# Hybrid decoder layer on one core: weight and block splits on VectorE, block sums among the products, and earlier loads of the linear attention's values

## The chip, the cores and the metric

One core of a Trainium2 chip runs the whole layer. Its engines work side by side, each through its own list of instructions in order: TensorE (PE in the profile, its weight loads PEld) does matrix products, VectorE (DVE), ScalarE (ACT) and GpSimd (POOL) work on elements, SyncE (SP) issues the transfers. The metric is the device time of one execution in microseconds.

## The reference

One token mixer layer on 1024 tokens of width 1024, in float32:

```python
h = rms_norm(x, norm_w)
proj = h @ w_in          # a_q a_k a_v a_gate | b_q b_k b_v b_gate b_low | two merge gates
oa = sliding_window_attention(rope(a_q), rope(a_k), a_v, sinks) * silu(a_gate)
ob = rms_norm(gated_linear_attention(b_q, b_k, b_v, log_a), b_out_norm_w) * silu(b_gate)
merged = sigmoid(m_a) * (oa @ w_a_proj) + sigmoid(m_b) * (ob @ w_b_proj)
out = rms_norm(x + merged @ w_out, final_norm_w)
```

The sliding attention has 16 heads of 64 and a window of 128; the linear attention has 4 heads with keys of 128 and values of 256.

## The kernel before

**Precision.** Every float32 operand of a large product is split into a rounded part h (a cast, ScalarE) and a rest l = x - h (a subtraction on GpSimd or VectorE). A product is then three matmuls: h by h, h by l, l by h. `split_w` (L114) does this for weights, with the rest on GpSimd (L116); `split_block` (L904) for blocks of activations, with the cast in L905 and the rest in L906.

**Stages.** Norm, transposes and first merge gate tiles (to about 80 us); projections of b_q, b_k, b_v, b_gate and one merge gate by `seven_products` (to about 400); sliding attention (to about 725); linear attention for heads 0 and 1, `gla(0)`, and 2 and 3, `gla(2)` (to about 880), with projection tiles `ya` of w_a_proj as fillers; w_b_proj in four calls of `seven_products`, k = 0 to 3, 128 columns of each half of the output at a time (about 913 to 990); w_out in two calls, h = 0 and 1, with residual and final norm (to the end at 1106.7).

**seven_products** (L423) multiplies 2 x 2 blocks with seven products instead of eight. Its weights are the four quadrants a11 to a22; its activations come as seven block sums (`tset`), which are split beforehand. Before, each product has its own PSUM bank `sj`; VectorE carries the running sums u and u3 (`add`, L449 to 451) and closes the four quadrants (`give`, L458 to 462); after each quadrant `emit` follows: for w_b_proj `merge` (L983, L984: gate times value, plus ya), for w_out `norm`. The four weight sums (L479 to 482, in place) stand after the third product. `part` splits a weight quadrant right before its product. With 128 columns (w_b_proj) the products are those of `half_product` (L132), with 256 (w_out) those of `token_product` (L420).

**Block sums.** `block_sums` (L908) makes the seven sums and splits them: for ob, the linear attention's output, five of them before the last `ya` tiles and the other two (L951 to 956) right before w_b_proj; for w_b_proj's own output `merged` (tiles o4 to o7) all seven after the last call, L990 and 991, five with their rest on GpSimd.

**Linear attention.** Each `gla_step` loads its values vr (L820), splits them (vh by ScalarE, L768; vl by GpSimd, L769) and multiplies (L774). Its pools, `hpv` of vr, vh, vl among them, are opened after the sliding attention has closed its own. The gates bg (L800) are loaded by `gla_loads` ahead of the steps. Three merge gate tiles (`m_tiles`) are put among the sliding attention's last steps (L757), one more among the steps of gla(0): `pace` (L861) ties a group of three filler matmuls to each step.

**Order.** The order of each engine's list is made by the compiler's scheduler (`schedule_with_timeline_sim`), within the limits of pools, banks and `issue_after`.

## Time and profile before

| | us |
|---|---|
| runs: 1113.48, 1111.57, 1110.83; median | 1111.57 |
| profiled execution, own time | 1108.61 |
| span of the profiled execution | 1106.7 |
| PE busy | 1027.7 (93%) |
| DVE busy | 774.7 (70%) |
| POOL busy | 684.3 (62%) |
| ACT busy | 542.4 (49%) |
| mean granted TensorE clock | 0.979 |

The profile page divides the span into 40 slices of 27.7 us and gives each engine's busy share in tenths; the timeline lists single instructions with start, duration and, in brackets, how long the engine was idle before and which instruction ended that. A TensorE that is busy 93% of the time leaves 79 us of idle time, and on top of it the time at a lower granted clock.

### The profile page before, as it was taken

How to read it: one execution, taken by the hardware profiler on the slowest of the kernel's cores; microseconds unless marked ns; L12 is line 12 of the kernel's file. 1: busy time of each engine (PE TensorE's matmuls, PEld its weight loads, DVE VectorE, ACT ScalarE, POOL GpSimd, SP SyncE). 2: the span in 40 equal slices, each digit the busy share in tenths (PEclk: the TensorE clock that was granted, in tenths of full speed). 3: DMA queues.
4: the chain of work that ended last, by engine and by line, in shares of the span. 5: the costliest groups of instructions: out<-in, count | busy, mean ns of one | idle time of the engine just before them, and what ended most of it. 6: DMA issues, size and time to landing. Idle time of an engine off the chain costs nothing.

```text
span 1106.7 us, 16321 instructions
## 1 busy us (share of the span) xinstructions
PE 1027.7 (93%) x5544; PEld 873.9 (79%) x5544; DVE 774.7 (70%) x1241; ACT 542.4 (49%) x1312; POOL 684.3 (62%) x542
## 2 busy tenths in 40 slices
PE   4999999899999999999999999988999997994896
PEld 3786787688889997888888878777788886873896
DVE  5999887335564323489788788748755299899766
ACT  6345865333342214556666666557654143243444
POOL 6033555777985446578677567747744246688685
PEclk9999999999999999999999999989999998996999
DMA  7332443452424152222222124266644587531315
GB/s 256 87 114 68 144 160 119 142 188 95 131 98 127 65 153 60 65 69 68 68 83 78 49 77 132 82 206 206 219 148 152 194 253 238 171 115 57 124 50 190
DMA packets 126403, 141.07 MB, mean 127 GB/s; under 512 B 10352, under 2 KB 87024, under 8 KB 126320
## 3 DMA queue, kind: packets, MB, share of 16 engines
q1 hardware_dynamic: 126320, 140.03, 40.5%
q8 instruction: 44, 0.72, 0.3%
q14 instruction: 39, 0.32, 0.1%
HBM read 95.04 MB, written 40.24 MB: 122 GB/s over the span
## 4 chain that ended last, share of the span: by engine, by line
PE 60%; DVE 16%; POOL 8%; issue 6%; ACT 6%; DMA 4%; SPq 1%; POOLq 0%; DVEq 0%; ACTq 0%
PE pj L132 22%; PE sj L132 15%; PE sj L420 11%; POOL wl L116 3%; PE sc L689 2%; PE av L729 2%; PE av L774 2%; POOL b L906 2%; DMA r<-sp_ob 1%; POOL o L906 1%; ACT wh L115 1%; PE pt L713 1%; PE sc L774 1%; DVE u L523 1%; DMA gt<-sp_cum 1%
## 5 line engine op out<-in xcount | busy, mean ns | idle before, releaser
L132 PE MATMUL pj<-o,wh 128*128 128x512 f32 x1088 | 353.6, 400 | 2.5 <-ACT o L204 1.9
L132 PEld LDWEIGHTS pj<-o,wh 128*128 128x128 f32 x1088 | 200.8, 190 | 44.2 <-ACT o L204 2.1
L116 POOL TENSOR_TENSOR wl<-wr,wh 128x1024 fp32r<-128x1024 f32 (+1 forms) x76 | 167.4, 2211 | 107.5 <-ACT wh L115 99.7
L116 POOL TENSOR_TENSOR wl<-sraw,wh 128x512 fp32r<-128x512 f32 (+1 forms) x98 | 155.3, 1600 | 107.6 <-ACT wh L115 105.5
L132 PE MATMUL pj<-o,wl 128*128 128x512 f32 x544 | 215.6, 396 | 0.0
L132 PEld LDWEIGHTS pj<-o,wl 128*128 128x128 f32 x544 | 102.5, 188 | 21.6
L115 ACT CAST wh<-wr 128x1024 fp32r<-128x1024 f32 (+1 forms) x76 | 66.9, 890 | 93.3 <-PE pj L132 23.9
L132 PE MATMUL sj<-o,wh 128*128 128x512 f32 x352 | 110.5, 395 | 0.7 <-ACT u L467 0.7
L451 DVE TENSOR_TENSOR u<-u,sj 128x512 f32<-128x512 f32 x72 | 49.2, 683 | 72.0 <-PE sj L420 40.5
L115 ACT CAST wh<-sraw 128x512 fp32r<-128x512 f32 (+1 forms) x98 | 63.2, 678 | 57.2 <-PE sj L420 29.1
L420 PE MATMUL sj<-wh,b 128*128 128x256 f32 x320 | 62.2, 296 | 21.7 <-ACT b L905 14.7
L132 PEld LDWEIGHTS sj<-o,wh 128*128 128x128 f32 x352 | 65.9, 187 | 16.9 <-ACT u L467 1.1
L420 PEld LDWEIGHTS sj<-wh,b 128*128 128x128 f32 x320 | 52.8, 203 | 23.1 <-ACT b L905 15.1
L132 PE MATMUL sj<-o,wl 128*128 128x512 f32 x176 | 69.4, 394 | 0.0
L721 POOL TENSOR_TENSOR ch<-ph,cst 128x512 fp32r<-128x512 f32 x32 | 38.4, 1201 | 48.4 <-ACT ph L720 36.0
L704 ACT ACTIVATE sm<-sc,nm 128x129 f32<-128x129 f32 x128 | 45.8, 368 | 37.4 <-DVE nm L700 36.4
L132 PE MATMUL sj<-b,wh 128*128 128x512 f32 x160 | 51.0, 402 | 5.6 <-ACT wh L115 5.6
L420 PE MATMUL sj<-wh,o 128*128 128x256 f32 x320 | 55.2, 277 | 0.1
L420 PEld LDWEIGHTS sj<-wh,o 128*128 128x128 f32 x320 | 48.4, 188 | 0.4 <-ACT wh L115 0.3
L420 PE MATMUL sj<-wl,b 128*128 128x256 f32 x160 | 45.8, 293 | 0.2 <-POOL wl L116 0.2
L609 POOL TENSOR_TENSOR qs<-qs,sin 128x512 f32<-128x512 f32 x18 | 25.4, 1409 | 31.0 <-DMA qs<-q 31.0
L420 PE MATMUL sj<-wl,o 128*128 128x256 f32 x160 | 44.3, 277 | 0.0
(314 smaller groups left out, 2737.3 us busy)
## 6 DMA issues: line engine op xcount, KB each, us to landing
sraw<-in_w_in_dram SPq DMA_DIRECT2D x32, 512.0 KB, 4.0
wr<-in_w_in_dram SPq DMA_DIRECT2D x26, 512.0 KB, 4.0
r<-sp_ob SPq DMA_DIRECT2D x28, 256.0 KB, 4.3
qs<-q SPq DMA_DIRECT2D x72, 64.0 KB, 2.0
xt<-in_x_dram SPq DMA_DIRECT2D x8, 512.0 KB, 8.6
sp_ma<-gt SPq DMA_DIRECT2D x16, 256.0 KB, 2.0
sp_mb<-c SPq DMA_DIRECT2D x16, 256.0 KB, 2.0
gt<-sp_cum SPq DMA_DIRECT2D x16, 256.0 KB, 3.7
```

The source lines that it names most:

```text
L115: nc.scalar.copy(h, raw)
L116: nc.gpsimd.tensor_sub(l, raw, h.bitcast(F32))
L132: nc.tensor.matmul(p, a[:, k, :], b[:, k, :], start=start and k == 0 and y == 0, stop=stop and k == 3 and y == 2)
L420: nc.tensor.matmul(p, m[i][:, k, t * P : t * P + P], w[j][:, k, :], start=k == 0 and y == 0, stop=k == 3 and y == 2)
L451: nc.vector.tensor_add(o[b], like(u[b], o[b]), like(x[b], o[b]))
L609: nc.gpsimd.tensor_mul(qs, qs, sin[:, sl])
L689: nc.tensor.matmul(s[:, h * 256 : h * 256 + 256], lq, kk[kv][x][:, k0 : k0 + 2, :].rearrange("p n t -> p (n t)"), start=x == 0, stop=x == 1)
L704: nc.scalar.activation(sm[:, j, :], sel[j // 2][:, j % 2, :], AF.Exp, bias=nm[:, j : j + 1], accum_out=den[:, j : j + 1])
L721: nc.gpsimd.tensor_mul(ch, ph.bitcast(F32), leb)
L729: nc.tensor.matmul(av[:, b * 256 : b * 256 + 256], val[:, blk, kv, :], part[:, 2 * b : 2 * b + 2, :], start=y == 0, stop=y == len(terms) - 1)
L774: nc.tensor.matmul(p, a[i], b[j], start=start and y == 0, stop=stop and y == 2)
L906: (eng or nc.vector).tensor_sub(m[1][:, k, :], r, f(m, 0, k))
```

## The change

- `split_w` takes its rest engine from `rest`: GpSimd until the first `ya` tiles, VectorE from then on. The splits of blocks and the norm's multiplications by `fnw` are on VectorE, too.
- `seven_products` splits three weight quadrants first, makes the four weight sums right behind them, and splits the others one product ahead. Where an `order` is given (w_b_proj and w_out), products 3 and 5 add onto product 1's bank and 7 onto 4's; ScalarE copies the bank after 1, 3 and 5 (u1, u3, u5), and VectorE only closes the quadrants. Without it (the projections) the sums are those of before.
- `after` is called behind each product: `last_blocks` during k = 0 of w_b_proj, `sums` (merged's block sums, slices 0 to 2, slice 3 where ready) during k = 3.
- w_out's halves of rows are swapped, and the residual is added in `norm` for three of four quadrants.
- `hpv` is opened before the sliding attention; two merge gate tiles instead of three stand in its last steps, and two instead of one in gla(0), with six filler matmuls a step.

```diff
+    rest = [nc.gpsimd]
     def split_w(raw, h, l):
         nc.scalar.copy(h, raw)
-        nc.gpsimd.tensor_sub(l, raw, h.bitcast(F32))
+        rest[0].tensor_sub(l, raw, h.bitcast(F32))
...
+        w = {i: part(r, n) for i, r in ((1, a11), (2, a12), (6, a22))}
         nc.vector.tensor_add(a22, a21, a22)
         nc.vector.tensor_sub(a21, a11, a21)
         nc.vector.tensor_sub(a11, a22, a11)
         nc.vector.tensor_sub(a12, a12, a11)
-        add(u, u, product(a11, t2))
-        u3 = tiles("u3")
-        add(u3, u, product(a21, t3))
-        for b in range(nb):
-            nc.vector.tensor_add(c[b], c[b], like(u3[b], c[b]))
-            emit(c[b], 1, 0, b)
-        x = product(a22, t1)
-        add(u, u, x)
-        earlier(u3, 1, 1)
-        give(1, 1, u3, x)
-        earlier(u, 0, 1)
-        if not fine:
-            give(0, 1, u, product(a12, b22))
+        by = {1: (b11, a11), 2: (b21, a12), 3: (t2, a11), 4: (t1, a22), 5: (t3, a21), 6: (t4, a22), 7: (b22, a12)}
+        x, u = {}, {}
+        def like(p, o):
+            return p.rearrange("p (t c) -> p t c", t=2) if len(o.shape) == 3 else p
+        def product(i, b):
+            if n == P:
+                half_product(x[i][b], w[i], by[i][0], not order or i not in (3, 5, 7), not order or i not in (1, 3, 4))
...
+        def ahead(i):
+            if i not in w:
+                w[i] = part(by[i][1], n)
+        def alone(i, following=None):
+            ahead(i)
+            x[i] = [bank("sj") for b in range(nb)]
+            for b in range(nb):
+                product(i, b)
+            if following:
+                ahead(following)
...
+        for i in order:
+            ahead(i)
+            x[i] = x[{3: 1, 5: 1, 7: 4}[i]] if i in (3, 5, 7) else [bank("sj") for b in range(nb)]
+            if i == 7 and fine:
+                break
+            for b in range(nb):
+                product(i, b)
+            if i in (1, 3, 5):
+                u[i] = [u_pool.tile([P, 512], F32, name=f"u{i}") for b in range(nb)]
+                for b in range(nb):
+                    nc.scalar.copy(u[i][b], x[i][b])
+                    if i == 3 and early:
+                        early(u[i][b], 0, 1, b)
+            if i == 2:
+                give(0, 0, 1, 2)
+            if i in (4, 5) and 4 in x and 5 in u:
+                give(1, 1, 5, 4)
+            if i in (5, 6) and 6 in x and 5 in u:
+                give(1, 0, 5, 6)
+            if i == 7:
+                give(0, 1, 3, 7)
+            if after:
+                after(i)
...
+    hpv = c3.enter_context(pool_of(name="hpv", bufs=4))
...
-                for _ in range(3):
+                for _ in range(2):
...
-    pace += [steps[min(15, 2 + i)] for i in range(16 * len(fillers))]
+    pace += [steps[min(15, 2 + i // 2)] for i in range(16 * len(fillers))]
...
+    rest[0] = nc.vector
+    up_ = lctx.enter_context(pool_of(name="up2", bufs=2))
+    sr = lctx.enter_context(pool_of(name="sr2", bufs=2))
...
+    def last_blocks(i):
+        if i < 3:
+            for k in (2 * i - 2, 2 * i - 1):
+                r11, r12 = (raw_block(k, 0, th) for th in range(TH))
+                nc.vector.tensor_sub(r12, r12, r11)
+                split_block(ob[5], k, r12)
+        if i == 3:
+            for k in range(4):
+                split_block(ob[6], k, raw_block(k, 1, 1))
...
+    def sums(i):
+        y = {1: 0, 2: 1, 3: 3, 4: 5, 5: 4, 6: 2, 7: 6}[i]
+        mt[y] = block(y)
+        def diff(k):
+            t2s.append(rp.tile([P, 512], F32, name="r"))
+            nc.vector.tensor_sub(t2s[k], c12[k], c21[k])
+            nc.vector.tensor_sub(c11[k], c11[k], t2s[k])
+        if i == 2:
+            split_block(mt[1], 3, c11[3])
+        if i == 6:
+            split_block(mt[0], 3, c21[3])
+            nc.vector.tensor_sub(c21[3], c22[3], c21[3])
+            split_block(mt[5], 3, c21[3])
+        for k in range(3):
+            if i == 3:
+                nc.vector.tensor_sub(c21[k], c22[k], c21[k])
+                diff(k)
+            if i == 5:
+                nc.vector.tensor_sub(c22[k], c12[k], c22[k])
+            if i < 7:
+                split_block(mt[y], k, {0: c21, 1: c11, 2: c11, 3: t2s, 4: c22, 5: c21}[y][k])
+        if i == 7:
+            diff(3)
+            split_block(mt[3], 3, t2s[3])
+            split_block(mt[2], 3, c11[3])
+            nc.vector.tensor_sub(c22[3], c12[3], c22[3])
+            split_block(mt[4], 3, c22[3])
+            for k in range(4):
+                split_block(mt[6], k, c12[k])
...
+                       lambda a, th, b: mg[a][th][:, k, :], merge, range(1, 8), after={0: last_blocks, 3: sums}.get(k))
...
-            nc.sync.dma_start(w[i, a], w_out[i * 512 : i * 512 + 512, c : c + 256].rearrange("(k p) c -> p k c", p=P))
+            nc.sync.dma_start(w[i, a], w_out[512 - i * 512 : 1024 - i * 512, c : c + 256].rearrange("(k p) c -> p k c", p=P))
...
+            if a == 1 or th == 0:
+                residual(o, a, th, b)
...
-                    nc.gpsimd.tensor_mul(o[:, t, :], o[:, t, :], fnw[:, cs])
-        seven_products([[w[i, a] for a in range(2)] for i in range(2)], mt, 256, up_,
+                    nc.vector.tensor_mul(o[:, t, :], o[:, t, :], fnw[:, cs])
...
+                       (1, 2, 6, 3, 5, 4, 7) if h else (1, 2, 4, 6, 3, 5, 7), early=residual, fine=h == 1)
```

How the order moves, at three places. First SP, the transfers, before: end of the sliding attention (oa is its output, written to sp_oa; bg the gates and vr the values of the linear attention; wr weights; sp_ma merge gate tiles).

```order
L308 DMA sp_ma_72<-gt_7009 128x512
L741 DMA sp_oa_70<-oa_6740 128x512
L800 DMA bg_7098<-sp_bg_77 128x2x512
L308 DMA sp_ma_72<-gt_7037 128x512
L800 DMA bg_7110<-sp_bg_77 128x2x512
L820 DMA vr_7122<-sp_bv_76 128x256
L820 DMA vr_7162<-sp_bv_76 128x256
L820 DMA vr_7202<-sp_bv_76 128x256
L820 DMA vr_7249<-sp_bv_76 128x256
L800 DMA bg_7486<-sp_bg_77 128x2x512
```

Now, the same tiles vr stand at the beginning of the sliding attention, among the last writes of sp_bv and ahead of and among the rope's loads qs:

```order
L122 DMA wr_3937<-in_w_in_dram 128x8x128
L857 DMA vr_7076<-sp_bv_76 128x256
L857 DMA vr_7116<-sp_bv_76 128x256
L601 DMA sp_bv_76<-c_3606 128x2x256
L857 DMA vr_7156<-sp_bv_76 128x256
L857 DMA vr_7203<-sp_bv_76 128x256
L122 DMA wr_4227<-in_w_in_dram 128x8x128
L857 DMA vr_7250<-sp_bv_76 128x256
L857 DMA vr_7297<-sp_bv_76 128x256
L857 DMA vr_7344<-sp_bv_76 128x256
L646 DMA qs_3690<-q_3688 32x512 x4
```

and at the attention's end the list reads:

```order
L779 DMA sp_oa_70<-oa_6647 128x512
L779 DMA sp_oa_70<-oa_6759 128x512
L857 DMA vr_7464<-sp_bv_76 128x256
L837 DMA bg_7052<-sp_bg_77 128x2x512
L837 DMA bg_7064<-sp_bg_77 128x2x512
L837 DMA bg_7440<-sp_bg_77 128x2x512
L837 DMA bg_7452<-sp_bg_77 128x2x512
L857 DMA vr_7511<-sp_bv_76 128x256
```

So the first eight loads of vr have moved from behind bg to some 70 rows earlier; bg still stands behind the last write of sp_oa.

Second TensorE at the same place: pj are merge gate products, av with ph, pl, ch, cl the attention's last ones, L813 to 815 of the linear attention's first step (L850 to 852 now). Before:

```order
L132 MATMUL pj_6950<-o6_89,wl_6919 128x512
L132 MATMUL pj_6984<-o0_83,wh_6980 128x512
L132 MATMUL pj_6984<-o1_84,wh_6980 128x512
L132 MATMUL pj_6984<-o0_83,wl_6981 128x512
L729 MATMUL av_6782<-ph_6774,vv_3730 128x256
L132 MATMUL pj_6984<-o0_83,wh_6980 128x512
L132 MATMUL pj_6984<-o1_84,wh_6980 128x512
L729 MATMUL av_6724<-cl_6719,dv_3731 128x256
L729 MATMUL av_6724<-ph_6716,vv_3730 128x256
L729 MATMUL av_6724<-ch_6718,dv_3731 128x256
L729 MATMUL av_6724<-pl_6717,vv_3730 128x256
```

Now:

```order
L134 MATMUL pj_6969<-o6_89,wl_6938 128x512
L767 MATMUL av_6801<-ph_6793,vv_3749 128x256
L767 MATMUL av_6743<-cl_6738,dv_3750 128x256
L767 MATMUL av_6743<-ph_6735,vv_3749 128x256
L767 MATMUL av_6743<-ch_6737,dv_3750 128x256
L767 MATMUL av_6743<-pl_6736,vv_3749 128x256
L767 MATMUL av_6743<-cl_6738,dv_3750 128x256
L751 MATMUL pt_6840<-cst_97,sm_6818 128x128 x4
L767 MATMUL av_6801<-ch_6795,dv_3750 128x256
L767 MATMUL av_6801<-pl_6794,vv_3749 128x256
L767 MATMUL av_6801<-cl_6796,dv_3750 128x256
L767 MATMUL av_6801<-ph_6793,vv_3749 128x256
```

The merge gate matmuls that stood before and among the attention's last products are gone from there (they are fillers of gla(0) now).

Third VectorE at the end of w_b_proj and the start of w_out: o4 to o7 are merged's quadrants, b0 to b9 and o0 to o3 the split block sums, wr and wl weights. Before, behind the last quadrant of k = 3 (L461 and merge):

```order
L461 TENSOR_TENSOR o6_9495<-u_9983,sj_10098 128x512
L983 SCALAR_TENSOR_TENSOR o6_9495<-ym_10112,o6_9495 128x512
L984 TENSOR_TENSOR o6_9495<-o6_9495,yt_10113 128x512
L919 TENSOR_TENSOR t2_10153<-o7_9497,o4_9494 128x512
L917 TENSOR_TENSOR o4_9494<-o6_9495,o4_9494 128x512
L920 TENSOR_TENSOR o5_9496<-o5_9496,t2_10153 128x512
L924 TENSOR_TENSOR o6_9495<-o7_9497,o6_9495 128x512
L906 TENSOR_TENSOR b7_10129<-t2_10153,b6_10128 128x512
L906 TENSOR_TENSOR b5_10127<-o5_9496,b4_10126 128x512
L919 TENSOR_TENSOR t2_10161<-o7_9497,o4_9494 128x512
L920 TENSOR_TENSOR o5_9496<-o5_9496,t2_10161 128x512
L906 TENSOR_TENSOR b7_10129<-t2_10161,b6_10128 128x512
```

Now from the sum that closes quadrant (1,1) of k = 3 on:

```order
L459 TENSOR_TENSOR o7_9468<-u5_10113,sj_10076 128x512
L459 TENSOR_TENSOR o5_9467<-u5_10113,sj_10133 128x512
L940 TENSOR_TENSOR b9_10123<-o7_9468,b8_10122 128x512 x2
L940 TENSOR_TENSOR b5_10154<-o4_9465,b4_10153 128x512 x2
L1009 TENSOR_TENSOR r_10069<-o6_9466,o5_9467 128x512
L1023 TENSOR_TENSOR o7_9468<-o6_9466,o7_9468 128x512
```

and, after 10 more rows:

```order
L1050 TENSOR_TENSOR o5_9467<-o5_9467,yt_10148 128x512
L940 TENSOR_TENSOR b9_10123<-o7_9468,b8_10122 128x512
L1049 SCALAR_TENSOR_TENSOR o6_9466<-ym_10181,o6_9466 128x512
L940 TENSOR_TENSOR b5_10154<-o4_9465,b4_10153 128x512
L437 TENSOR_TENSOR wr_10223<-wr_10221,wr_10223 128x1024
L940 TENSOR_TENSOR b1_9999<-o5_9467,b0_9998 128x512
L1050 TENSOR_TENSOR o6_9466<-o6_9466,yt_10182 128x512
```

Before, all block sums of merged stand behind the last merge. Now most of slices 0 to 2 stand among the products (b9, b5 and b3 are late ones of them), and the split of b1, slice 3, which w_out's first product needs, is the 24th instruction behind the sum L459 (rows with x2 counted twice). From the first instruction of k = 0 to that sum VectorE has 112 instructions, two of them of 128x1024.

179 lines of the change are left out of this document (80 added, 99 removed).

## The prediction

> **What bounds the kernel now.** I read the 40 slices first, because they show where TensorE is not full.
>
> ```profile
> PE   4999999899999999999999999988999997994896
> DVE  5999887335564323489788788748755299899766
> POOL 6033555777985446578677567747744246688685
> PEclk9999999999999999999999999989999998996999
> ```
>
> TensorE is near full everywhere, so the kernel is bound by it, except at the start (slice 0), in slices 26 and 27 (about 720 to 775 us, the end of the sliding attention and the first half of the linear attention), slice 33 (913, start of w_b_proj) and slices 36 and 37 (1000 to 1050, start of w_out). VectorE is full in the last two. Second I read TensorE's timeline there for what ended each wait; the bracket gives idle time and releaser.
>
> ```profile
> 734.23 0.58 PE L774 MATMUL av<-vh,ath 128*128 128x256 f32 x1 [4.11 <-ACT vh L768]
> 919.46 2.07 PE L132 MATMUL sj<-b,wh 128*128 128x512 f32 x4 [5.64 <-ACT wh L115]
> 993.67 0.51 PE L420 MATMUL sj<-wh,b 128*128 128x256 f32 x2 [2.21 <-DVE u L451]
> 1014.01 0.79 PE L420 MATMUL sj<-wh,b 128*128 128x256 f32 x2 [12.64 <-ACT b L905]
> 1018.37 1.01 PE L420 MATMUL sj<-wh,b 128*128 128x256 f32 x3 [3.57 <-DVE b L906]
> 1027.85 0.50 PE L420 MATMUL sj<-wh,b 128*128 128x256 f32 x2 [2.03 <-ACT b L905]
> 1029.54 0.58 PE L420 MATMUL sj<-wh,b 128*128 128x256 f32 x1 [1.19 <-DVE b L906]
> ```
>
> Seven waits, 31.4 us. Third, what a wait costs behind itself, from windows of 5 us (window, PE, PEld, DVE, ACT, POOL busy, then PEclk):
>
> ```profile
> 735.00:740.00 5.00, 5.00 (x27) 4.87 (x26) 2.12 (x6) 3.46 (x12) 3.68 (x7) 0.56 1.06 330
> 750.00:755.00 5.00, 4.58 (x23) 3.95 (x23) 4.08 (x9) 3.28 (x10) 4.08 (x8) 0.69 0.39 123
> 920.00:925.00 5.00, 5.00 (x16) 3.92 (x15) 5.00 (x5) 2.20 (x4) 2.64 (x2) 0.63 0.89 262
> 1020.00:1025.00 5.00, 5.00 (x34) 5.00 (x33) 4.87 (x8) 2.48 (x4) 0.00 (x0) 0.73 0.00 0
> 1030.00:1035.00 5.00, 5.00 (x33) 5.00 (x33) 4.15 (x6) 2.95 (x4) 3.16 (x1) 0.70 0.07 15
> ```
>
> After each the granted clock is low for a window: 5 x (1 - clock) = 2.2, 1.55, 1.85, 1.35 and 1.5 us lost. The Trainium skill's page "TensorE: Matmul & The Clock Gate" (section "Why this matters for your kernels") says that only idle gaps over about 3 us bring the half clock back. The trace agrees behind 4.11 and 5.64, but the low windows at 750 and 1030 stand behind pairs of waits of which none is longer than 2.03; by the rule the new waits under 2 us that I find below cost no clock, and the sum stands; by those two windows they cost about 1.5 us, and the sum would be 1088.5.
>
> Fourth, why VectorE is late at 1000 to 1030:
>
> ```profile
> 1009.37 8.40 POOL L906 TENSOR_TENSOR o<-o,o 128x512 fp32r<-128x512 f32 x5
> 1031.84 4.57 POOL L116 TENSOR_TENSOR wl<-wr,wh 128x1024 fp32r<-128x1024 f32 x1 [12.39 <-ACT wh L115]
> ...
> 1011.55 1.75 DVE L920 TENSOR_TENSOR o<-o,t 128x512 f32<-128x512 f32 x1
> 1020.03 0.69 DVE L920 TENSOR_TENSOR o<-o,t 128x512 f32<-128x512 f32 x1
> 1020.68 0.69 DVE L906 TENSOR_TENSOR b<-t,b 128x512 fp32r<-128x512 f32 x1
> 1021.41 0.69 DVE L906 TENSOR_TENSOR b<-o,b 128x512 fp32r<-128x512 f32 x1
> 1022.02 0.68 DVE L919 TENSOR_TENSOR t<-o,o 128x512 f32<-128x512 f32 x1
> ```
>
> The same instruction of L920 takes 1.75 us while GpSimd runs its subtraction and 0.69 while GpSimd idles (nothing of its between 1019.5 and 1031.8). With GpSimd idle one starts every 0.60 to 0.73 (1020.68, 1021.41, 1022.02). This is the reading on which the forecast rests: GpSimd's work is paid twice, on its own engine and on VectorE.
>
> **The change, part by part.**
>
> *Work moved off GpSimd.* What leaves it, from its groups after 782 us (count, busy, mean ns):
>
> ```profile
> L116 POOL TENSOR_TENSOR wl<-wr,wh 128x512 fp32r<-128x512 f32 x28 | 45.3, 1634 | 33.1 <-ACT wh L115 28.5 <-DMA sp_t<-yt 4.6
> L906 POOL TENSOR_TENSOR b<-o,b 128x512 fp32r<-128x512 f32 x12 | 20.5, 1737 | 0.0
> L906 POOL TENSOR_TENSOR o<-o,o 128x512 fp32r<-128x512 f32 x8 | 13.0, 1658 | 0.0
> L1037 POOL TENSOR_TENSOR o<-o,fnw 128x256 f32<-128x256 f32 x24 | 22.0, 941 | 2.8 <-ACT zj L1033 2.8
> L906 DVE TENSOR_TENSOR b<-r,b 128x512 fp32r<-128x512 f32 x16 | 13.1, 849 | 3.7 <-ACT b L905 3.7
> L451 DVE TENSOR_TENSOR u<-u,sj 128x512 f32<-128x512 f32 x24 | 16.4, 681 | 13.8 <-PE sj L420 7.7 <-PE sj L132 6.1
> ```
>
> All four GpSimd groups, four more splits of blocks and 19 weight splits of 128x1024 go to VectorE, and GpSimd is nearly silent from w_b_proj on. On VectorE a moved 128x512 costs 0.60 to 0.73 where GpSimd needed 1.6 to 1.7; I take 0.60, and for 128x1024 twice that, 1.2. Against that, VectorE loses 24 of the sums of the 0.681 row, which the product's bank takes over; ScalarE gets 8 copies, hidden, since it is busy only 25.3 of 72 us in the row of 919.46:991.47 below.
>
> *Start of w_b_proj.* The 5.64 us wait ends with a weight cast, which waits for VectorE's weight sums:
>
> ```profile
> 917.01 1.75 DVE L481 TENSOR_TENSOR wr<-wr 128x512 f32<-128x512 f32 x1
> ...
> 919.46:991.47 72.01, 71.95 (x306) 58.58 (x306) 64.95 (x72) 25.32 (x43) 50.78 (x31) 0.97 0.56 172
> ```
>
> Such a sum at 0.60 instead of 1.75 gives 1.1 us back each, the splits ahead of it as well, and the sums now stand right behind the first splits, one product before they are needed. The second set of late block splits (L953 to 956) also moves behind w_b_proj's first products. I let the wait go with its clock: 5.64 + 1.85 = 7.5 saved, less 1.1 for one sum that may still be waited for, **6.4** (bounds 3 and 7.5: the loads of the blocks are not faster than before).
>
> *Inside w_b_proj.* Before, VectorE did 72 instructions beside TensorE's 72 us. Now merged's block sums stand among them: by the order, 112 instructions from the first of k=0 to the sum that closes quadrant (1,1) of k=3, 110 x 0.60 + 2 x 1.2 = 68 us beside the same 72. It just fits, but the margin is 4 us and VectorE works in order, so each wait for a product delays what is queued behind it, and product 7 now cannot start before that sum has read the bank that it adds to. I charge 2 us (bounds 0 and 6).
>
> *Start of w_out.* Between that closing sum and the last split of the first w_out operand (b1, slice 3) stand 24 instructions: 22 x 0.60 + 2 x 1.2 = 15.6 us. TensorE has, in the same time, product 7 and 28 matmuls of w_out's second product, at the pace of these two rows:
>
> ```profile
> 722.71 3.27 PE pj L132 x14
> 1036.46 47.41 PE sj L420 x398
> ```
>
> 12 x 0.2336 + 28 x 0.119 = 6.1 us. So TensorE waits 15.6 - 6.1 = 9.5 us in one piece, then runs cold for 1.7 (mean of the five windows above). Before: 2.21 + 12.64 + 3.57 + 2.03 + 1.19 = 21.6 idle, and behind it the clock: 1.35 and 1.5 from the windows at 1020 and 1030, and 0.6 for the five matmuls at 1014.01 and 1018.37, at half pace: 25.1. Saved 25.1 - 2 - 9.5 - 1.7 = **11.9** (bounds 4, where VectorE's interval is 0.73 and the charge 6, and 21, where TensorE finds other work). The rest of w_out has some 550 matmuls, 65 us, beside about 53 us of VectorE at the same prices (an estimate over its order): hidden. The norm's multiplications by fnw, on VectorE now, are among these 53; were that cover gone they would cost 24 x 0.4 = 10.
>
> *Attention's end and linear attention.* The chain of waits there, and the queue that issues its loads:
>
> ```profile
> 705.72 4.45 PE pj L132 x19
> ...
> 711.59 0.48 ACT ph L720
> 728.50 5.25 DMA vr<-sp_bv
> ...
> 727.09 0.37 SPq L800 DMA_DIRECT2D bg<-sp_bg  x1
> 728.50 2.31 SPq L820 DMA_DIRECT2D vr<-sp_bv  x4
> ...
> 745.00:785.00 40.00, 33.27 (x201) 27.54 (x200) 34.73 (x88) 27.56 (x89) 31.25 (x44) 0.96 0.67 218
> ```
>
> The values vr come 5.25 us after an issue at 728.50, behind the gates bg on SP. Loaded some 300 us earlier, they take the 4.11 us and its 2.2 of clock with them: 6.3. In the 40 us behind, TensorE idles 6.7 and loses 1.55 of clock at 750; one more filler tile (doubled pace, 6 matmuls or 1.4 us a step instead of 0.7) covers some 4 of these. What is late next: the tile that is gone stood in the attention's last chain. TensorE's other work is done at 710.2, and the next product needs ph, ready at 712.1: 1.9. The transposes and the bank behind it want 1.2 and 1.5 more by the same order, and the first step's own norm chain about 1.4, since its pt now follows after 15 matmuls. Together 6.0 (the last three are estimates from durations of casts and norm steps there): 6.3 + 4 - 6.0 = 4.3, and with the clock at 750 **6** (bounds 1 and 10). The bg loads still wait for the attention's last output; VectorE's first product with bg stands 13 instructions behind that output, so it may wait 0 to 2 us, in the bounds.
>
> The early loads of vr stand on SP ahead of the attention's first rope loads. Six issues take 6 x 0.58 = 3.5 (from the row of four, 2.31), if SP doesn't idle there anyway: 0 to 3.5, taken as 0, since the rope loads wait for a cast of ScalarE. The pair stage keeps its order on all engines: 0. Tail: 0.1 to 0.8 less, taken 0.3.
>
> Sum: 6.4 + 11.9 + 6 + 0.3 = 24.6. The profiled execution took 1108.6 us (span 1106.7 and 1.9 around it); 1084.0 then. The median of the runs shown, 1111.57, is 3.0 above that execution: **1087**.
>
> **Rivals.**
>
> *VectorE becomes the bound.* If its dependent sums start every 0.68 instead of 0.60, 136 of them cost 11 us more, of which the margin of 4 hides some: 7 late: 1094. For it: 24.73 of 25 us busy at 975 to 1000. Against: most neighbours in the new order work on different tiles.
>
> ```profile
> 975.00:1000.00 25.00, 22.74 (x126) 19.58 (x125) 24.73 (x18) 10.88 (x20) 25.00 (x14) 1.00 0.31 106
> ```
>
> *The slower side.* VectorE's slowness isn't GpSimd's doing and stays. Then 136 moved and old instructions at the 0.849 mean of the mixed group cost 136 x 0.25 = 34 us, less 4 of margin: 30 us against the 24.6 saved, 5 slower: 1117. It decides from an interval of 0.60 + (24.6 + 4) / 136 = 0.81. Against it the same instruction at 1.75 and 0.69. The Trainium skill's page "Perfetto Trace Analysis" (section "Optimizing Scalar/DVE Operations") advises the opposite of this change, to offload a saturated VectorE even to GpSimd, though it warns that the two share a read port; by the advice the move would end here, by the warning and by the rows at 1011.55 and 1020.03 it does not.
>
> *Nothing is won at the attention's end.* The wait for vr becomes one for ph, the banks and bg, all 6 us of it: 1093.
>
> *More is won.* TensorE's order at w_out has enough beside the splits, so that the 9.5 shrink to 3 and don't let the clock fall: 1079.
>
> **How the numbers follow.** Forecast (1081 to 1092) 0.5; VectorE the bound (to 1100) 0.2; nothing at the attention's end 0.1; more won (down to 1073) 0.14; slower side 0.04, change without effect 0.02. 1073 to 1100 leaves out about 2 in 10. A measurement of this kernel can tell some 0.3% (3.3 us) from no change; faster by more 0.93, within 0.03, slower 0.04.
>
> **What would show it.** VectorE's 128x512 subtractions near 0.69 from 913 us on and GpSimd silent there; no TensorE wait for a weight cast near 905; one wait of 6 to 11 us for a split or cast of b near 990 to 1005, in place of 12.64 and 3.57; no wait for vh, but for ph, at the attention's end. Wrong if VectorE's subtractions stay over 0.8, or if TensorE waits inside w_b_proj for VectorE by over 6 us.

## The result, and the profile after

| | before | changed |
|---|---|---|
| runs, us | 1110.33, 1110.83, 1111.57, 1113.48 | 1083.87, 1085.11, 1085.45, 1085.83 |
| median, us | 1111.20 | 1085.28 |
| profiled execution (span), us | 1108.61 (1106.7) | 1085.83 (1084.0) |
| PE busy, us | 1027.7 | 1023.3 |
| POOL busy, us | 684.3 | 528.1 |
| mean granted TensorE clock | 0.979 | 0.989 |

The ratio is 0.9762, 95% interval 0.9744 to 0.9779: faster by 25.9 us, 24.6 forecast. The same four rows of the 40 slices (27.1 us each now) as for the kernel before:

```profile
PE   4999999989999999999999999989999999996996
DVE  5999887534655421378878888877866379889786
POOL 5123555687897446756677766577853100000002
PEclk9999999999999999999999999999999999998999
```

GpSimd is silent from slice 32 (870 us) to the last, TensorE's dip at 720 to 775 is small, and of the two weak slices at 1000 to 1050 one is left (slice 36, 976 to 1003). TensorE's waits of over 1 us where the prediction's seven stood, and two others, on the changed kernel's timeline (two more, of 1.1 and 1.0 at 784 and 790, are left out):

```profile
435.69 1.12 PE L684 MATMUL pt<-cst,q 128*128 128x128 f32 x4 [4.04 <-ACT q L681]
...
717.67 0.38 PE L767 MATMUL av<-ph,vv 128*128 128x256 f32 x1 [1.05 <-ACT ph L758]
728.77 0.36 PE L811 MATMUL av<-vh,ath 128*128 128x256 f32 x1 [1.21 <-ACT kth L805]
919.51 0.74 PE L134 MATMUL sj<-b,wh 128*128 128x512 f32 x2 [1.12 <-ACT wh L117]
983.78 0.38 PE L422 MATMUL sj<-wl,b 128*128 128x256 f32 x1 [1.61 <-DVE wl L118]
990.99 0.39 PE L422 MATMUL sj<-wh,b 128*128 128x256 f32 x1 [2.12 <-DVE b L940]
998.19 0.52 PE L422 MATMUL sj<-wh,b 128*128 128x256 f32 x2 [2.09 <-ACT b L939]
1001.08 0.58 PE L422 MATMUL sj<-wh,b 128*128 128x256 f32 x1 [2.38 <-DVE b L940]
```

The wait for vh is gone. The one of 5.64 is 1.12. The 12.64 and 3.57 have become four of about 2. But at 435.69, the start of the sliding attention, a wait has grown from 0.90 to 4.04: there something was lost. The same wait before:

```profile
430.86 0.66 PE L646 MATMUL pt<-cst,q 128*128 128x128 f32 x4 [0.90 <-ACT q L643]
```

Where the time went, by the moment at which TensorE reaches the same amount of work (counted from its timelines, one profiled execution each; both hold the same 5544 matmuls, 4464 of them ahead of w_b_proj's first):

| TensorE reaches | before | changed | ahead by | since the row above |
|---|---|---|---|---|
| the end of its 2000th matmul (the attention's first tile of q) | 413.2 | 414.9 | -1.7 | -1.7 |
| the attention's first softmax transposes | 465.6 | 471.8 | -6.2 | -4.5 |
| the first matmul of w_b_proj | 888.7 | 885.4 | 3.3 | +9.5 |
| 240 matmuls of w_b_proj | 968.1 | 958.4 | 9.6 | +6.3 |
| 320 matmuls of w_b_proj | 986.3 | 977.3 | 9.0 | -0.6 |
| 200 matmuls of w_out | 1042.0 | 1018.4 | 23.5 | +14.5 |
| its last matmul | 1097.6 | 1075.3 | 22.3 | -1.2 |
| end of the span | 1106.7 | 1084.0 | 22.7 | +0.4 |

The 1.7 us of the first row are scatter between executions: in the fourteen profiled ones of this document TensorE ends its 2000th matmul between 411.9 and 415.2.

### The profile page after: what moved, and what is told of

Same layout as the page of the kernel before. It is cut to its first block, busy times and chain, and to the rows that moved or that the text cites. A ratio compares the mean times of both kernels' runs of the same rounds, so it can differ in the third digit from the quotient of the medians.

```text
span 1084.0 us, 16202 instructions
## 1 busy us (share of the span) xinstructions
PE 1023.3 (94%) x5544; PEld 870.1 (80%) x5544; DVE 768.1 (71%) x1312; ACT 546.9 (50%) x1320; POOL 528.1 (49%) x447
## 4 chain that ended last, share of the span: by engine, by line
PE 47%; DVE 14%; DMA 4%; POOL 4%; ACT 4%; issue 4%; SPq 0%; POOLq 0%; DVEq 0%; ACTq 0%
PE pj L134 16%; PE sj L422 14%; PE sj L134 9%; PE av L811 2%; PE sc L727 1%; DMA r<-sp_ob 1%; DVE b L940 1%; PE av L767 1%; ACT sm L742 1%; DVE oa L778 1%; DVE sm L750 1%; DVE sc L735 1%; DVE qb L708 1%; DVE nm L738 1%; PE sc L811 1%
## 5 line engine op out<-in xcount | busy, mean ns | idle before, releaser
L134 PEld LDWEIGHTS pj<-o,wh 128*128 128x128 f32 x1088 | 202.0, 191 | 43.6 <-ACT o L206 2.1
L117 ACT CAST wh<-wr 128x1024 fp32r<-128x1024 f32 (+1 forms) x76 | 66.9, 892 | 84.4 <-PE sj L422 23.5
L146 POOL TENSOR_SCALAR rstd<-zs 128x1 f32<-128x1 f32 x8 | 2.7, 334 | 213.4 <-DVE zs L1067 213.0
L118 POOL TENSOR_TENSOR wl<-wr,wh 128x1024 fp32r<-128x1024 f32 x29 | 72.0, 2482 | 34.8 <-ACT wh L117 31.6
L476 DVE TENSOR_TENSOR u<-u,sj 128x512 f32<-128x512 f32 x48 | 32.8, 684 | 55.1 <-PE sj L422 32.5
L459 DVE TENSOR_TENSOR c<-u,sj 128x512 f32<-128x512 f32 x48 | 32.7, 681 | 27.9 <-DMA sp_bq<-c 8.6
```

What stands on the lines that cost most here:

```text
L117: nc.scalar.copy(h, raw)
L118: rest[0].tensor_sub(l, raw, h.bitcast(F32))
L134: nc.tensor.matmul(p, a[:, k, :], b[:, k, :], start=start and k == 0 and y == 0, skip_group_check=True, stop=stop and k == 3 and y == 2)
L459: nc.vector.tensor_add(o, like(u[i][b], o), like(x[j][b], o))
L476: nc.vector.tensor_add(o[b], u[i][b], x[j][b])
```

## The experiments

Each run was compared with the kernel before on its own chip; there the latter's median was 1109.2 (first four runs), 1113.2 (next four) and 1111.1 (last four), so ratios are compared, not microseconds.

| run | median, us | ratio to before | 95% interval |
|---|---|---|---|
| changed kernel | 1085.28 | 0.9762 | 0.9744 to 0.9779 |
| values' pool as before | 1095.57 | 0.9880 | 0.9835 to 0.9924 |
| values in mid-attention | 1077.56 | 0.9720 | 0.9700 to 0.9740 |
| rests on GpSimd | 1104.25 | 0.9956 | 0.9942 to 0.9971 |
| before, rests on VectorE | 1106.43 | 0.9976 | 0.9957 to 0.9995 |
| sums written at the end | 1086.96 | 0.9771 | 0.9728 to 0.9813 |
| fillers 3 and 1 | 1086.03 | 0.9770 | 0.9736 to 0.9804 |
| running sums on VectorE | 1096.17 | 0.9861 | 0.9823 to 0.9900 |
| values mid, one group first | 1080.91 | 0.9732 | 0.9699 to 0.9765 |
| values mid, splits as needed | 1071.80 | 0.9656 | 0.9633 to 0.9680 |
| before, rests on VectorE, pool open | 1095.72 | 0.9865 | 0.9840 to 0.9889 |
| before, values mid | 1100.57 | 0.9910 | 0.9886 to 0.9934 |
| late block sums ahead | 1082.16 | 0.9746 | 0.9723 to 0.9769 |

### What the early loads win and cost

Two runs: the changed kernel with the values' pool opened behind the attention again,

```diff
-    hpv = c3.enter_context(pool_of(name="hpv", bufs=4))
...
-    hpa, bp1, bpe, bps, bp, hp = (c3.enter_context(pool_of(name=nm, bufs=n)) for nm, n in (
+    hpa, bp1, bpe, bps, hpv, bp, hp = (c3.enter_context(pool_of(name=nm, bufs=n)) for nm, n in (
```

> The changed kernel, but the pool of the linear attention's values is opened after the sliding attention again, as before. Theory (early loads delay the attention's start by about 6 us and save about as much at the linear attention's start): the wait of 4.04 us at 432 shrinks to about 0.9, a wait of about 4 us for vh returns at the linear attention's start, total 1084 to 1088. Rival (the early loads win clearly more than they cost): 1090 or more. Rival (they only cost): about 1079.

and the changed kernel with the pool early, but the loads held back on SP:

```diff
+            late.append(nc.sync.dma_start(sp_oa[i * P : (i + 1) * P, th * 512 : th * 512 + 512], oa).ins)
...
-        nc.sync.dma_start(vr, sp_bv[t * P : t * P + P, hd * BV : (hd + 1) * BV])
+        with tc.issue_after(late[6]):
+            nc.sync.dma_start(vr, sp_bv[t * P : t * P + P, hd * BV : (hd + 1) * BV])
```

> The changed kernel, but SP may issue the loads of the values only behind the write of the seventh half of the sliding attention's output (in its middle), the pool still being opened ahead. Theory (the early loads hold up the first rope transfers through SP's and ScalarE's queues): wait at 432 back to about 0.9, no wait for vh at the linear attention's start, total about 1079, 6 us below the changed kernel. Rival (the wait at 432 comes from the pool's place in memory or from the order of other work): stays at 1085.

The second came out as its theory had it: 0.9720, the best so far, with 0.91 us at the attention's start and no wait for vh. The first came out at 0.9880; the rival "win clearly more than they cost" held. Its timeline at the linear attention's start and its SP issues:

```profile
733.00 0.58 PE L810 MATMUL av<-vh,ath 128*128 128x256 f32 x1 [11.14 <-ACT vh L804]
...
714.13 11.06 SPq L778 DMA_DIRECT2D sp_oa<-oa  x2
727.03 0.89 SPq L836 DMA_DIRECT2D bg<-sp_bg  x2
727.96 1.88 SPq L856 DMA_DIRECT2D vr<-sp_bv  x4
```

The loads are issued at the same moment as before (727.96 against 728.50), behind the attention's last output, but TensorE is ready 8 us sooner, since one filler tile is gone from there. So the wait is 11.14, not 4.11: with the tile gone the early loads are needed. From the first softmax transposes to w_b_proj's first matmul TensorE takes 428.0 us here and 413.6 in the changed kernel; at the attention's start the late pool wins 4.6. The way in which they cost, in the changed kernel at the attention's start (SP and ScalarE), and below it the same instructions before:

```profile
416.69 1.72 SPq L857 DMA_DIRECT2D vr<-sp_bv  x3
418.46 1.87 SPq L646 DMA_DIRECT2D qs<-q  x3
...
415.45 0.75 ACT L805 CAST vh<-vr 128x256 fp32r<-128x256 f32 x2 [5.17 <-DMA vr<-sp_bv]
416.81 0.81 ACT L805 CAST vh<-vr 128x256 fp32r<-128x256 f32 x2 [0.61 <-DMA vr<-sp_bv]
417.52 0.58 ACT L642 COPY q<-pj 128x512 f32<-128x512 f32 x1
```

```profile
413.81 2.51 SPq L608 DMA_DIRECT2D qs<-q  x4
...
413.20 0.59 ACT L604 COPY q<-pj 128x512 f32<-128x512 f32 x1 [4.61 <-PE pj L132]
```

ScalarE's copy of q, which the first rope loads wait for, stands behind four casts of vh, and these wait for vr: 417.52 instead of 413.20. SP's rope loads stand behind three loads of vr that wait for a buffer to come free: 418.46 instead of 413.81. Of those 4.65 us, 1.7 are the scatter of the table's first row, for the copy waits for the 2000th matmul; the other 3 are the queues, and TensorE's wait grows by as much (0.90 to 4.04). The granted clock of 0.66 at 435 to 440 makes the rest of the table's 4.5 (5 x 0.34 = 1.7). From the 2000th matmul to the first softmax transposes the eight profiled executions without early loads at the attention's start need 52.4 us, and the six with them 57.0 to 58.4.

The third run of this group takes the same step alone, on the kernel before.

> The kernel before with only the loads of the linear attention's values moved to the middle of the sliding attention. Theory: the wait of 4.1 us for vh goes with its 2.2 us of clock, nothing is lost at the attention's start, 1103 to 1106 (ratio 0.993 to 0.995). Rival (something else is late there, such as the gates' loads): 1109 or more.

It gave 0.9910 (10 us), more than the 6 expected. From the attention's first softmax transposes to w_b_proj's first matmul, before, in this run and in the changed kernel (the first number behind the comma is TensorE's busy time):

```profile
465.58:888.66 423.08, 406.64 (x2231) 343.13 (x2230) 309.72 (x646) 249.08 (x796) 265.61 (x247) 0.99 0.40 123
466.79:879.88 413.09, 402.35 (x2231) 339.91 (x2230) 307.57 (x649) 247.22 (x796) 263.55 (x247) 1.00 0.41 126
471.83:885.38 413.55, 403.03 (x2232) 340.44 (x2230) 316.21 (x656) 249.05 (x792) 247.17 (x236) 1.00 0.41 127
```

In this run the stretch is 10.0 us shorter: idle time falls by 5.7 (16.4 to 10.7), and TensorE's busy time for the same matmuls by 4.3, at a higher granted clock. Expected were 4.1 and 2.2. How much of the difference is scatter stays open: three profiled executions of the changed kernel's list of instructions (two of them are runs below) need 411.5 to 414.5 us for this stretch.

### The moved filler tile

```diff
-                for _ in range(2):
+                for _ in range(3):
...
-    pace += [steps[min(15, 2 + i // 2)] for i in range(16 * len(fillers))]
+    pace += [steps[min(15, 2 + i)] for i in range(16 * len(fillers))]
```

> The changed kernel, but three filler tiles in the sliding attention's end and one in gla(0), paced as before. Theory of the prediction (the moved tile uncovers about as much as it covers): 1083 to 1088, with the waits for ph and kth at 717 and 728 smaller and the waits of the linear attention's steps at 745 to 785 larger. Rival (the second tile in gla(0) is what wins there): 1089 to 1093. Rival (it costs): 1081 or less.

0.9770, not to be told from the changed kernel. TensorE has no wait over 0.5 us at 715 to 750 there, but four of 1.0 to 2.0 between 753 and 778. From the first softmax transposes to w_b_proj's first matmul it needs 411.3 us, beside those 411.5 to 414.5. As with the prediction's 4 and 1.55 against 6.0, the tile covers about as much in one place as in the other; what it needs is that vr is there early.

### VectorE and GpSimd

The changed kernel with the rests back on GpSimd:

```diff
-    rest[0] = nc.vector
...
-        split_block(ob[3], k, t2)
+        split_block(ob[3], k, t2, nc.gpsimd)
...
-                    nc.vector.tensor_mul(o[:, t, :], o[:, t, :], fnw[:, cs])
+                    nc.gpsimd.tensor_mul(o[:, t, :], o[:, t, :], fnw[:, cs])
```

(and so for five of merged's seven block sums).

> The changed kernel, but the weight rests, the block rests that were GpSimd's before and the norm's multiplications stay on GpSimd. Theory (GpSimd's work slows VectorE, and its moving away is what shortens the start of w_out): VectorE's 128x512 subtractions at up to 1.7 us again, waits at the start of w_b_proj and w_out grow, total 1098 to 1108. Rival (the place of the block sums among the products is what wins, not the engine): 1083 to 1090, since VectorE would have less to do.

0.9956: 21 us of the 26 are gone. Its VectorE, GpSimd and TensorE at w_out's start:

```profile
976.88 1.75 DVE L1008 TENSOR_TENSOR r<-o,o 128x512 f32<-128x512 f32 x1
981.90 4.49 DVE L1050 TENSOR_TENSOR o<-o,yt 128x512 f32<-128x512 f32 x2
986.31 0.68 DVE L1009 TENSOR_TENSOR o<-o,r 128x512 f32<-128x512 f32 x1
...
978.05 5.04 POOL L940 TENSOR_TENSOR o<-o,o 128x512 fp32r<-128x512 f32 x3
987.11 1.61 POOL L940 TENSOR_TENSOR b<-o,b 128x512 fp32r<-128x512 f32 x1 [1.28 <-ACT b L939]
...
988.70 0.79 PE L422 MATMUL sj<-wh,b 128*128 128x256 f32 x2 [11.03 <-ACT wh L117]
```

Sums of the same shape are at 1.75 and more beside GpSimd and at 0.68 in its pause at 986, and a wait of 11 us is back, for a weight's cast this time. At w_b_proj's start, however, this run has no wait over 1.4 us. So GpSimd's work alone does not make the 5.64 there. Over w_b_proj's first 240 matmuls it costs something all the same: 76.6 us, against 79.4 before and 73.1 in the changed kernel. The kernel before with only the engine changed tells the other half:

```diff
-        nc.gpsimd.tensor_sub(l, raw, h.bitcast(F32))
+        rest[0].tensor_sub(l, raw, h.bitcast(F32))
...
     ya_tiles((0, 1, 2))
+    rest[0] = nc.vector
...
-    block_sums(mt, [(k, [mg[i][th][:, k, :] for i in range(2) for th in range(TH)]) for k in range(4)], zw, (0, 1, 4, 5, 6))
+    block_sums(mt, [(k, [mg[i][th][:, k, :] for i in range(2) for th in range(TH)]) for k in range(4)], zw, ())
```

(likewise for ob's block sums and the norm's multiplications).

> The kernel before with only the engine changed: weight rests from the first ya tiles on, all block rests and the norm's multiplications on VectorE. Theory of contention: VectorE near 0.6 us an instruction from 880 us on, the wait of 5.6 us at w_b_proj's start down to 0 to 2, the wait of 12.64 at w_out's start down to some 4 to 8, total 1093 to 1102. Rival (VectorE becomes the bound without the new places of the sums): 1108 or more.

0.9976: the expected 1093 to 1102 missed, the rival's time nearly met, though not for its reason:

```profile
923.65 1.65 PE L134 MATMUL sj<-b,wh 128*128 128x512 f32 x3 [7.42 <-ACT wh L117]
...
1010.10 0.80 PE L422 MATMUL sj<-wh,b 128*128 128x256 f32 x2 [5.38 <-ACT b L907]
```

The wait at w_out's start fell from 12.64 to 5.38, as the theory has it, but the one at w_b_proj's start rose from 5.64 to 7.42. Ahead of the weights' casts on ScalarE's list, and of the weight sums on VectorE's, stands work of ob's two late block sums that waits for its loads:

```profile
920.94 0.62 ACT L907 CAST o<-r 128x512 fp32r<-128x512 f32 x1 [4.75 <-DMA r<-sp_ob]
...
920.14 0.69 DVE L957 TENSOR_TENSOR r<-r 128x512 f32<-128x512 f32 x1 [1.09 <-DMA r<-sp_ob]
```

From 240 matmuls of w_b_proj to 200 of w_out TensorE needs 73.9 us before, 65.9 here, 73.8 with all but the engine, 60.0 in the changed kernel: the engine alone is worth 8, the rest of the change alone nothing, both 14.

### What lets the sums come early

The block sums written behind w_b_proj's last call again, on VectorE:

```diff
-                       lambda a, th, b: mg[a][th][:, k, :], merge, range(1, 8), after={0: last_blocks, 3: sums}.get(k))
+                       lambda a, th, b: mg[a][th][:, k, :], merge, range(1, 8), after={0: last_blocks}.get(k))
+    all_sums()
```

> The changed kernel, but merged's block sums are written behind the last w_b_proj call again (all on VectorE); the scheduler may still draw single ones forward. Theory (with VectorE near 0.6 us an instruction, their place is worth what lies between the engine change alone and the changed kernel at w_out's start, about 5 us): about 1088 to 1092. Rival (the bank that takes over sums explains that difference): 1084 to 1086.

This run did not test what it was made for: the scheduler gave every engine the same list as in the changed kernel, but for the buffers' numbers. It is a second measurement of the changed kernel, on another chip (0.9771 beside 0.9762), and says that the place in the source does not set the order. Something else must, and the suspect was the pool of the temporaries, one buffer in a pool that opens when w_b_proj's own has closed. That pool can hold back only the sums that need the temporary and what follows from them. Before, too, six of merged's sums and the first splits on GpSimd ran ahead of the last merge (the first sum, L917, at 981.7, the last merge at 1005.6), so what is said of the order ahead of the prediction, that all block sums stood behind it, is too strong; the sums of L919, into the temporary, start at 1007.1. The kernel before with the engine changed and that pool replaced by rp2, which here stays open until merged's block sums are done:

```diff
-    rp = rctx.enter_context(pool_of(name="rp2", bufs=7))
+    rp = rctx.enter_context(pool_of(name="rp2", bufs=7, side="right"))
...
-            t2 = tmp.tile([P, 512], F32, name="t2", bufs=1)
+            t2 = rp.tile([P, 512], F32, name="r")
...
-    rctx.close()
...
+    mt = blocks() + last_blocks()
+    block_sums(mt, [(k, [mg[i][th][:, k, :] for i in range(2) for th in range(TH)]) for k in range(4)], rp, ())
+    rctx.close()
     yctx.close()
```

> The kernel before with the rests on VectorE (as in the run with only the engine changed), and the temporaries of merged's block sums from the pool of seven buffers, kept open through w_b_proj, instead of one buffer in a pool that opens behind w_b_proj's last merge. Theory (the pool kept the sums behind the last merge, since the scheduler draws them forward where it can): w_out's start as in the changed kernel, 4 to 6 us below the run with only the engine changed, 1099 to 1103. Rival (the pool does not hold them): 1104 to 1108.

0.9865, 11 us below the engine alone (0.9976), more than expected. The sums into the temporary (L921 in both runs), with the engine alone and here (shortest, median and longest duration in ns, then first and last start in us):

```profile
L921 DVE TENSOR_TENSOR t<-o,o x4: 691/698/705, 1014.6 to 1027.3; 128x512 f32<-128x512 f32 x4
L921 DVE TENSOR_TENSOR r<-o,o x4: 690/692/692, 984.9 to 1017.6; 128x512 f32<-128x512 f32 x4
```

So the pool had held them, and three of the four come early now. But that is not where the 11 us are: TensorE needs 64.1 instead of 65.9 us over the stretch above, far from the 60.0 of the changed kernel, and w_out's start still has waits of 2.96, 1.54, 4.37 and 1.50. Most of the 11 comes from w_b_proj's start, where the 7.42 us wait is gone: 71.6 us for the first 240 matmuls instead of 80.9. That start was the object of one more run, the changed kernel with the two late block sums ahead of w_b_proj:

```diff
+    for i in (1, 2, 3):
+        last_blocks(i)
     ring = [0]
...
-                       lambda a, th, b: mg[a][th][:, k, :], merge, range(1, 8), after={0: last_blocks, 3: sums}.get(k))
+                       lambda a, th, b: mg[a][th][:, k, :], merge, range(1, 8), after={3: sums}.get(k))
```

> The changed kernel, but the two late block sums of ob are written ahead of w_b_proj again, as before, instead of among its first products. Theory (these splits, which wait for their loads, stood ahead of the weight sums on VectorE and made the 5.64 us wait): a wait of 3 to 6 us for a weight cast returns at w_b_proj's start, ratio to the kernel before 0.979 to 0.984. Rival (the weight sums' place alone, or VectorE's speed, took the wait away): 0.975 to 0.978.

0.9746, with a wait of 2.14 us. That is close to the rival's time, but like the run with the sums at the end, this one did not test what it was made for: on every engine its instructions stand in the order of the changed kernel. It is a third measurement of that kernel, and the three (0.9762, 0.9771, 0.9746) say how far two ratios can lie apart for nothing. So the theory is not refuted by it, and the traces of the two runs on the kernel before fit it: with the engine alone VectorE's third weight sum (L483, at 920.75) stands behind three of the four late block sums (L957), with the pool open (at 915.24) behind one. But with the rests on GpSimd it stands behind three, too, without a wait over 1.4 us, so the order is not the whole cause. In the two runs on the kernel before the source of all this is the same; what differs are the pools. By the order in which they open, up2 and sr2, for w_b_proj's copies and weights, no longer lie where the loads of ob have to be finished first, and so it is in the changed kernel and in the run with the rests on GpSimd. The engine is not what takes the wait away: it is there with the engine alone (7.42) and not with all but the engine. That leaves the pools, and on the kernel before they do take it away. The open-pool run changes two things about them, and no run parts these or tries them on the changed kernel.

### The running sums

Each product in its own bank, the sums on VectorE (24 more additions, 16 fewer copies):

```diff
-            x[i] = x[{3: 1, 5: 1, 7: 4}[i]] if i in (3, 5, 7) else [bank("sj") for b in range(nb)]
+            x[i] = [bank("sj") for b in range(nb)]
...
+                        nc.vector.tensor_add(u[i][b], u[i - 2][b], x[i][b])
...
+                total(u[3], 3, 4)
```

> The changed kernel, but in w_b_proj and w_out every product has its own bank and VectorE adds the running sums (three more additions a call and block, 24 in all, 8 fewer copies on ScalarE). Theory (VectorE is the bound from w_b_proj to w_out's start): 12 more additions of 0.6 us in w_b_proj come out nearly whole there, total 1089 to 1093. Rival (TensorE covers them): 1085 to 1087.

0.9861 (1096.17; its profiled execution 1091.75): the loss is 11 us by the ratios. From w_b_proj's first matmul to its last TensorE needs 202.0 us, 189.9 in the changed kernel: 4 of these 12 are lost in w_b_proj's first 240 matmuls, 3 up to 200 of w_out, 5 behind. One wait of 8.25 us for a running sum stands at w_out's start, where the small ones were, and one for a closing sum near the end:

```profile
990.61 0.77 PE L422 MATMUL sj<-wh,b 128*128 128x256 f32 x2 [8.25 <-DVE u L522]
...
1076.85 0.79 PE L422 MATMUL sj<-wh,o 128*128 128x256 f32 x2 [4.17 <-DVE o L544]
```

VectorE is the bound here: additions that the bank takes over are time won. The rival that TensorE covers them falls.

### Order on VectorE at w_out's start

From the run with the values in mid-attention on, two orders for the same work. First everything that w_out's first products do not need, its weight sums included, behind what they need (`issue_after` on the splits of mt[0] and mt[5], slice 3):

```diff
+        with tc.issue_after(behind) if behind else nullcontext():
+            w[6] = part(a22, n)
+            nc.vector.tensor_add(a22, a21, a22)
...
+            first.append(split_block(mt[5], 3, c21[3]).ins)
+            with tc.issue_after(first[1]):
+                splits(6)
+                splits(5)
```

> The kernel with the values loaded in the middle of the sliding attention, and in addition VectorE may do the block splits that w_out's first products do not need, and w_out's weight sums, only behind the splits that they do need; the work is the same. Theory (TensorE waits at w_out's start for VectorE's order, about 8 of the 15.6 us between the closing sum and the split of b1 being work for later products): b1's split comes some 8 us after that sum, the waits at w_out's start fall from 8 to 9 us to 2 to 5, total 1071 to 1074. Rival (VectorE's whole load counts, so the waits come back at the next products): 1076 to 1079.

0.9732, nothing won over 0.9720: the four small waits became one of 2.15 us and a long one for product 4's weights, whose rests I had put behind splits of blocks.

```profile
1000.01 0.58 PE L422 MATMUL sj<-wl,o 128*128 128x256 f32 x1 [8.22 <-DVE wl L118]
```

That is a fault of that order and no answer on the load. Second, the weights left where they were, and the splits in the order of the products (1, 2, 4; then 6; then the rest):

```diff
+            with tc.issue_after(first[1]):
+                splits(6)
...
+                diff(3)
+                first.append(split_block(mt[2], 3, c11[3]).ins)
+            with tc.issue_after(first[2]):
+                split_block(mt[3], 3, t2s[3])
+                splits(5)
```

> The kernel with the values loaded in the middle of the sliding attention, and block splits in the order in which w_out's products need them (those for product 6 behind those for 1, 2 and 4, the rest behind these); w_out's weight sums stay where the scheduler puts them, since holding them back made one wait of 8.2 us for the weights of product 4. Theory (TensorE waits at w_out's start for VectorE's order): b1's split about 10 us behind the closing sum instead of 15.6, waits at w_out's start 3 to 5 us instead of 8 to 9, ratio to the kernel before 0.965 to 0.969. Rival (VectorE's whole load up to there counts): 0.971 to 0.974, as with the values alone.

0.9656, the best of all: 38 us below the kernel before, 10.6 thousandths below the changed kernel. Its VectorE from the closing sum to b1's split, TensorE's waits at 960 to 1003 (us in total, times, longest), and a window:

```profile
976.16 1.28 DVE L459 TENSOR_TENSOR o<-u,sj 128x512 f32<-128x512 f32 x2
986.61 0.68 DVE L942 TENSOR_TENSOR b<-o,b 128x512 fp32r<-128x512 f32 x1
...
PE sj L422 <- DVE wl L118: 1.7, 1, 1.7
PE sj L422 <- ACT wh L117: 1.5, 1, 1.5
PE sj L422 <- ACT u L520: 0.4, 1, 0.4
...
975.00:1000.00 25.00, 22.78 (x166) 21.84 (x167) 24.79 (x34) 10.94 (x17) 0.00 (x0) 0.93 0.24 77
```

10.5 us instead of 15.5, 3.6 us of listed waits, and VectorE as full as ever: what TensorE waited for was VectorE's order, not its load.

## Why the prediction was right, point by point

**VectorE's speed.** As forecast. Groups of the changed kernel from 880 us on, and its VectorE at w_out's start:

```profile
L118 DVE TENSOR_TENSOR wl<-wr,wh 128x512 fp32r<-128x512 f32 x28 | 18.6, 682 | 0.7 <-ACT wh L117 0.7
L940 DVE TENSOR_TENSOR b<-r,b 128x512 fp32r<-128x512 f32 x22 | 14.4, 681 | 1.0 <-ACT b L939 0.8
...
984.85 1.27 DVE L459 TENSOR_TENSOR o<-u,sj 128x512 f32<-128x512 f32 x2
1000.35 0.67 DVE L940 TENSOR_TENSOR b<-o,b 128x512 fp32r<-128x512 f32 x1
...
975.00:1000.00 25.00, 17.02 (x94) 14.53 (x92) 25.00 (x39) 11.35 (x20) 0.00 (x0) 0.90 0.20 65
1000.00:1025.00 25.00, 23.92 (x186) 23.92 (x187) 20.36 (x29) 12.30 (x22) 0.00 (x0) 0.89 0.44 145
```

0.68 us each, 39 instructions in 25 us where 18 stood before. The slower side (an interval of 0.81) and the dependent sums at 0.68 fell: the 24 instructions behind the closing sum took 15.5 us. The Trainium skill's page "GPSIMD Engine Reference" (section "8. Key points") says that GpSimd shares its SBUF interfaces with VectorE and contends with instructions of two SBUF inputs; the 1.75 and 0.68 of the run with the rests on GpSimd agree.

**w_out's start.** 11.9 forecast with 2 charged inside w_b_proj; 14.5 - 0.6 = 13.9 measured. From the closing sum at 984.85 to b1's split at 1000.35 are 15.5 us, 15.6 forecast. The form was different: I had one wait of 9.5, and it came as four (1.61, 2.12, 2.09, 2.38: 8.2 in all), since TensorE's list has pieces of other products between. The clock's loss was larger, 2.5 and 2.75 us by the two windows instead of 1.7.

**w_b_proj's start.** 6.4 forecast, 6.3 measured. Of the two reasons that I gave, VectorE's speed does not take the wait away (7.42 with the engine alone, none over 1.4 with all but the engine), though it has a part in the time: 3.5 of the 6.3 are lost again with the rests on GpSimd. The other, the weight sums ahead of the late block splits, is not shown; on the kernel before it was a change of the pools, which I had not named, that took the wait away.

**The attention's end.** 6 forecast, 9.5 measured (the three executions named above scatter by 3). The clock was about right: 2.2 + 1.55 forecast, and TensorE's busy time fell by 3.6 (406.6 to 403.0). Idle time was mis-sized: I had 4.1 + 4 saved and 6.0 of new waits, 2.1 in all, and it fell by 5.9 (16.4 to 10.5). Of the new waits only those for ph and kth are over 1 us at 715 to 750, with 1.05 and 1.21.

**The attention's start.** Here the prediction's step was wrong: six early issues (seven in the trace) "taken as 0, since the rope loads wait for a cast of ScalarE". That copy itself was queued behind casts that wait for the early loads, and 4.5 us were lost, past the bound of 3.5 that I had named. The 3.5 by which the term above was too small made most of it up; that was luck, and without it the forecast would have been some 4 too low. The run with the values in mid-attention shows the loss to be avoidable.

**Fillers, running sums, tail.** The moved tile is neutral, about as costed. The 24 sums were worth more than I said of them, 11 to 12 us by the run that puts them back. The tail gave 0.4 (0.3 forecast), but w_out behind its 200th matmul lost 1.2, which I had put at nothing.

**The total.** 24.6 forecast, 22.8 between the two profiled executions (with 1.7 of scatter against the change), 25.9 between the medians.

## What to carry to other kernels

Price an early load by every instruction that it issues on every engine's list: its cast and its buffer's wait stand ahead of work that is due (in the middle of the stage, not at its start, the same loads gave 5 us more here, by the ratios). Where two engines slow each other, work moved between them is not priced by its own duration, and neither the move nor the new order has to show a gain alone (8 and 0 us here, 14 together). When a full engine holds up another, look first at what the other needs next: the same load in the order of need gave 7 us more, by the ratios. And before a run is read as a test, compare the lists that were executed: two of these runs changed the source and no instruction's place.

## What the runs showed of the hardware

A low granted clock follows not only waits over 3 us: in the changed kernel, whose waits at w_out's start are at most 2.4 us, the window of 975 to 1000 has a mean clock of 0.90, the next 0.89; in the run with the splits as needed, with waits of at most 1.7 us, it is 0.93. In the changed kernel four waits of 1.6 to 2.4 us within 20 us go with about 5 us of lost clock in these two windows (25 x 0.10 + 25 x 0.11).

GpSimd does not slow all of VectorE's instructions. Before, with GpSimd busy in all of 975 to 1000 us, the sums that read a PSUM bank take 0.67 to 0.68 us (L451 at 990.17 and 992.94), and those of the same shape beside them with both inputs in SBUF 1.67 to 2.25 (990.77 to 995.85).
